# Dilated attention in an encoder layer: heads kept apart by zeros in q's tiles, k whole as hi and lo, staging in two buffers

## The chip, the cores and the metric

The kernel runs on one core of a Trainium2 chip. The metric is the device time of one execution in microseconds, the median of several runs. Engines are named as in the profile: PE is the matrix engine (TensorE), PEld its weight loads, DVE the vector engine, ACT the scalar engine, POOL is GpSimd, SP the engine that issues most DMAs.

## What is computed

One encoder layer over 2048 positions of width 1024, all in float32: a mixer of three parallel head groups, cross-attention into 256 memory tokens, and a gated feed-forward block with a convolution of width 3. The change lies in the third head group of the mixer, the dilated window attention. It has three groups of two heads of 64 columns each, with dilations 1, 4 and 16; each query sees the keys at most 64 steps of its dilation away:

```python
def _dilated_window_attention(q, k, v, rel_table_g, dilation, radius):
    ...
    logits = jnp.einsum('bdnqhe,bdnkhe->bdnhqk', qs, kb).astype(jnp.float32) * (E ** -0.5)
    logits = logits + bias[None, None, None].astype(jnp.float32)
    logits = jnp.where(valid[None, None, :, None], logits, NEG_INF)
    lse = jax.nn.logsumexp(logits, axis=-1)
    p = jnp.exp(logits - lse[..., None]).astype(v.dtype)
    out = jnp.einsum('bdnhqk,bdnkhe->bdnqhe', p, vb).reshape(B, dilation, Lp, H, E)[:, :, :L]
    ...
```

The three groups' outputs are merged with weights from their softmax denominators.

## The kernel before

The program runs four stages one after the other. `mix_in` projects the input and writes q, k and the pooling channels, transposed, to `zt` in DRAM and v to `vt`. `mixer` does the dilated attention and, between its pieces, the projections of the memory tokens (`kv_step`). `OutProj` and `xattn` follow, then `Ffn`. Every product is made from float32 operands that are split into a rounded part (hi, type F32R) and its remainder (lo); `mm3` (lines 111 to 117) adds the three products hi*hi, hi*lo and lo*hi in PSUM.

In `mixer` the attention is cut into 12 units: three groups, dilation 16 (g = 2) first, then 4, then 1, with four units of 512 queries each. A unit holds 512 keys for g = 2 and 640 (64 more at each side) for the others. `unit` (line 894) loads and splits a unit's operands, and `block` (line 956) computes 128 queries against 256 keys, for two heads; for g = 2 a block is two sets of 128 queries against 128 keys. So a unit has four blocks (two for g = 2), and there are 32 blocks of 256-wide products and 8 blocks of twice as many 128-wide ones. One unit ahead is prepared while a unit's blocks run (line 1072); its split tiles alternate between two pools, `un[0]` and `un[1]`, by the unit's number.

How `unit` splits its operands: the transposed k of two heads arrives as one tile of 128 partitions, head 0 on partitions 0 to 63, head 1 on 64 to 127. For each head, `kh` is made to hold that head's hi twice, on both halves of the partitions: ACT writes one half (line 924), DVE copies the other (line 925, through `copy`, line 873), and DVE makes the remainder `kl` on 64 partitions (line 926). `q` holds, for each head, hi on the lower half and lo on the upper half (lines 930 to 934), with one more DVE copy for head 1. So one product over 128 rows gives hi*hi and lo*hi together, and a second over 64 rows gives hi*lo:

```python
nc.tensor.matmul(pl[:, a, ws], q[:, a, qs], kh[:, a, ks], start=True, stop=False)
nc.tensor.matmul(pl[:, a, ws], q[lo, a, qs], kl[:, a, ks], start=False, stop=True)
```

After them DVE adds the bias and finds the row's maximum (line 975), ACT takes the exponent (980), PE transposes (985), ACT and DVE split the result (988, 989), PE multiplies by v (999), and ACT and DVE gather the output (1003, 1004). `merge` (1008) joins the three groups.

`stage` (line 907) loads a tile through SP's queue; its pool `m_stg` has one buffer for each of the tags sk, sq and sv, so the next unit's load waits until the last reader of this unit's tile is done. `kv_step` (line 1121) loads weights by SP as well (line 1088), and POOL splits them (`split_w`, lines 95 and 99). The framework orders the instructions of each engine itself, by a simulated time line, so their order is not that of the source; each engine then runs its own list strictly in order.

Of the kernel before, what the change touches and what calls it, by code (L numbers as in the profile page):

```python
# [9 lines left out]
F32 = mybir.dt.float32  # L10
F32R = mybir.dt.float32r
I32 = mybir.dt.int32
AF = mybir.ActivationFunctionType
ALU = mybir.AluOpType
# [4 lines left out]
P = 128  # L19
# [807 lines left out]


MJ = 2
KD_ENG, QD_ENG = "dve", "dve"  # L830
KVH, KVL = ("pool",), ("pool",)
OEB, LGB, PHB = 6, 4, 2
UJ = (3, 2, 1)
# [3 lines left out]
def mixer(cx, zt, vt, yt, tt, mem, mem_t, gm, w_kv, w_qt, w_o, gx, a_d, vo_d, open_proj):  # L837
# [4 lines left out]
    tc, nc = cx.tc, cx.nc  # L842
    with ExitStack() as es:
        ek = ExitStack()
        pool = cx.pools(ek)
# [3 lines left out]
        kvp = pool("m_kv", 2, side="right")  # L849
        psk = pool("m_psk", 2, space=PSUM, side="right")  # L850
        pool = cx.pools(es)
        stg = pool("m_stg", 1)
        midp = pool("m_mid", 2)
        un = [pool("m_un0", 1)]
        one = pool("m_one", 1)
# [8 lines left out]
        pso = pool("m_pso", 2, space=PSUM)  # L864


        og = {g: dr.tile([S, 132], F32, name=f"og{g}") for g in (1, 2)}

        def copy(eng, out, src, f):
            if eng == "act":  # L870
                nc.scalar.activation(out, src, AF.Copy, scale=f)
            else:
                (nc.gpsimd if eng == "pool" else nc.vector).tensor_scalar(out, src, f, 1.0, op0=ALU.mult, op1=ALU.mult)

        def mask_tiles(g):

# [17 lines left out]
        def unit(g, u, masks):  # L894

            d = DIL[g]
            L = S // d
            pad = 0 if d == 16 else 64  # L900
            n = 512 + 2 * pad
            c0 = 512 * u

            z0 = pad if (g == 1 or u == 0) else 0
            z1 = n - pad if (g == 1 or u == 3) else n

            def stage(b, pd, tag):
                w = 512 + 2 * pd
                y0, y1 = (z0, z1) if pd else (0, w)
                t = stg.tile([P, w], F32, name="stage", tag=tag)  # L910
                for lo, hi in ((0, y0), (y1, w)):
                    if lo < hi:
                        nc.vector.memset(t[:, lo:hi], 0.0)
                nc.sync.dma_start(t[:, y0:y1], zt[b, :, c0 - pd + y0:c0 - pd + y1])
                return t


            lo, up = slice(0, 64), slice(64, P)
            heads = (lo, up)
            s = stage(5 + g, pad, "sk")  # L920
            kh = un[u % 2].tile([P, 2, n], F32R, name="kh", tag="kh")
            kl = un[u % 2].tile([64, 2, n], F32R, name="kl", tag="kl")
            for a, h in enumerate(heads):
                nc.scalar.activation(kh[h, a], s[h], AF.Copy)
                copy(KD_ENG, kh[heads[1 - a], a], s[h], 1.0)
                nc.vector.tensor_tensor(kl[:, a], s[h], kh[h, a].bitcast(F32), op=ALU.subtract)
            s = stage(2 + g, 0, "sq")
            q = un[u % 2].tile([P, 2, 512], F32R, name="q", tag="q")
            for a, h in enumerate(heads):
                nc.scalar.activation(q[h, a], s[h], AF.Copy, scale=0.125)  # L930
                if a:
                    copy(QD_ENG, q[lo, a], s[h], 0.125)
                nc.vector.scalar_tensor_tensor(q[up, a], s[h], 0.125, q[h, a].bitcast(F32),
                                               op0=ALU.mult, op1=ALU.subtract)

            nt = n // P
            s = stg.tile([P, nt, P], F32, name="stage", tag="sv")
            rows = vt[:, g * P:(g + 1) * P].rearrange("(l r) c -> r l c", r=d)
            if g == 2:
                nc.sync.dma_start(s, rows[4 * u:4 * u + 4].rearrange("r l c -> l r c"))  # L940
            else:
                rows, k0 = rows[u if g == 1 else 0], (0 if g == 1 else c0) - pad
                t0, t1 = int(z0 > 0), nt - (z1 < n)
                if t0:
                    nc.vector.memset(s[:64, 0], 0.0)
                    nc.sync.dma_start(s[64:, 0], rows[:64])
                if t1 < nt:
                    nc.vector.memset(s[64:, t1], 0.0)
                    nc.sync.dma_start(s[:64, t1], rows[L - 64:])
                nc.sync.dma_start(s[:, t0:t1], rows[k0 + t0 * P:k0 + t1 * P].rearrange("(t p) c -> p t c", p=P))  # L950
            v = un[u % 2].tile([P, nt, 2, 2, 64], F32R, name="v", tag="v")
            s4 = s.rearrange("p t (a e) -> p t a e", a=2)
            nc.scalar.activation(v[:, :, :, 0], s4, AF.Copy)
            nc.vector.tensor_tensor(v[:, :, :, 1], s4, v[:, :, :, 0].bitcast(F32), op=ALU.subtract)

            def block(i, oe):

                pl = psl.tile([P, 2, 256], F32, name="pl", tag="pl")
                if g == 2:

                    parts = [(slice((2 * i + j) * P, (2 * i + j + 1) * P),) * 2 + (slice(j * P, (j + 1) * P), j)
                             for j in range(2)]
                    mk = masks[1]
                else:
                    parts = [(slice(i * P, (i + 1) * P), slice(i * P, (i + 2) * P), slice(0, 256), 0)]
                    first, last = (i == 0, i == 3) if g == 1 else (u == 0 and i == 0, u == 3 and i == 3)
                    mk = masks[0 if first else 2 if last else 1]
                for a in range(2):
                    for qs, ks, ws, _ in parts:
                        nc.tensor.matmul(pl[:, a, ws], q[:, a, qs], kh[:, a, ks], start=True, stop=False)  # L970
                        nc.tensor.matmul(pl[:, a, ws], q[lo, a, qs], kl[:, a, ks], start=False, stop=True)
                lg = lgp.tile([P, 2, 256], F32, name="lg", tag="lg")
                for a in range(2):
                    for _, _, ws, j in parts:
                        nc.vector.tensor_tensor_reduce(out=lg[:, a, ws], in0=pl[:, a, ws], in1=mk[:, a, ws], scale=-1.0,
                                                       scalar=3e38, op0=ALU.add, op1=ALU.min,
                                                       accum_out=oe[:, j, 128 + a:129 + a])
                for a in range(2):
                    for _, _, ws, j in parts:
                        nc.scalar.activation(lg[:, a, ws], lg[:, a, ws], AF.Exp, scale=-1.0,  # L980
                                             bias=oe[:, j, 128 + a:129 + a], accum_out=oe[:, j, 130 + a:131 + a])
                pt = psp.tile([P, 4, P], F32, name="pt", tag="pt")
                for a in range(2):
                    for t in range(2):
                        nc.tensor.transpose(pt[:, 2 * a + t], lg[:, a, t * P:(t + 1) * P], cx.ident)
                ph = wk.tile([P, 4, P], F32R, name="ph", tag="ph", bufs=PHB)
                pl_ = wk.tile([P, 4, P], F32R, name="pl_", tag="pl_", bufs=PHB)
                nc.scalar.activation(ph, pt, AF.Copy)
                nc.vector.tensor_tensor(pl_, pt, ph.bitcast(F32), op=ALU.subtract)
                m = len(parts)  # L990

                po = pso.tile([P, 2, 2, 2, 64], F32, name="po", tag="po")
                for j in range(m):
                    for a in range(2):
                        ts = [j] if g == 2 else [0, 1]
                        for t in ts:
                            vi = 2 * i + t if g == 2 else i + t
                            for p in (ph, pl_):
                                nc.tensor.matmul(po[:, j, a].rearrange("p h e -> p (h e)"), p[:, 2 * a + t],
                                                 v[:, vi, a].rearrange("p h e -> p (h e)"),  # L1000
                                                 start=t == ts[0] and p is ph, stop=t == ts[-1] and p is pl_)
                o4 = oe[:, :, 0:128].rearrange("p m (a e) -> p m a e", a=2)
                nc.scalar.activation(o4, po[:, :m, :, 0], AF.Copy)
                nc.vector.tensor_tensor(o4, o4, po[:, :m, :, 1], op=ALU.add)

            return block
# [102 lines left out]
        for i in range(2):  # L1109
# [4 lines left out]
            for k in range(4):  # L1114
# [3 lines left out]
                                               op0=ALU.mult, op1=ALU.subtract)  # L1118
# [299 lines left out]
def body(tc, x_t, gmix, w_t, b_t, w_v, b_v, w_a, b_a, v_g, w_s, b_s, rel, oh, mrow, pw, pb, psc, edge, invw, mem, mem_t, gm, w_kv, w_qt,  # L1418
         w_o, gmem, w_out, b_out, b_o, w_up, b_up, conv, w_down, b_down, gffn, gfin, out):
    with tc.tile_pool(name="const", bufs=1) as const, tc.tile_pool(name="scratch", bufs=1, space=DRAM) as dr:  # L1420
# [15 lines left out]
        def open_proj():  # L1436
# [4 lines left out]
            return proj[0].chunk  # L1441

        mixer(cx, zt, vt, yt, tt, mem, mem_t, gm, w_kv, w_qt, w_o, gmem, a_d, vo_d, open_proj)
        with late, ExitStack() as ef, ExitStack() as ep:
            def ffn():
# [55 lines left out]
```

## Time and profile before

| | us |
|---|---|
| median of 3 runs | 2616.39 (2615.14 to 2619.52) |
| the profiled execution | 2622.29 |
| its span in the trace | 2620.5 |

| stretch of the trace (us) | what runs | PE busy | DVE busy | granted clock |
|---|---|---|---|---|
| 0 to 430 | input projections, gating, pooling | 412.8 | 287.7 | 0.98 to 1.00 |
| 430 to 712 | dilated attention and the memory projections | 251.1 | 227.0 | 0.88 |
| 712 to 1010 | output projection, cross-attention begins | 286.8 | 192.4 | 0.97 to 0.99 |
| 1010 to 2620 | the rest of it and the feed-forward block | 1569.6 | 1162.2 | 0.99 |

The granted clock is the share of full speed that the chip allowed PE, on average over the stretch; it has two levels, 1.2 and 2.4 GHz, so 0.88 is a mixture of 0.5 and 1. A matmul's duration includes its way through the array, so two neighbours overlap in the records; what a matmul costs is the distance from its start to the next one's start.

### The profile page before, as it was taken

How to read it: one execution, taken by the hardware profiler on the slowest of the kernel's cores; microseconds unless marked ns; L12 is line 12 of the kernel's file. 1: busy time of each engine (PE TensorE's matmuls, PEld its weight loads, DVE VectorE, ACT ScalarE, POOL GpSimd, SP SyncE). 2: the span in 40 equal slices, each digit the busy share in tenths (PEclk: the TensorE clock that was granted, in tenths of full speed). 3: DMA queues.
4: the chain of work that ended last, by engine and by line, in shares of the span. 5: the costliest groups of instructions: out<-in, count | busy, mean ns of one | idle time of the engine just before them, and what ended most of it. 6: DMA issues, size and time to landing. Idle time of an engine off the chain costs nothing. (4 is left out here: it accounts for less than half of the span.)

```text
span 2620.5 us, 33979 instructions
## 1 busy us (share of the span) xinstructions
PE 2520.3 (96%) x12390; PEld 2137.0 (82%) x12390; DVE 1869.3 (71%) x2736; ACT 1010.1 (39%) x1536; POOL 1017.4 (39%) x841
## 2 busy tenths in 40 slices
PE   8999998899999899998999999989999999999998
PEld 6988896787778799987788888767888888888886
DVE  7666748878763967667788888785888887646453
ACT  4222112556321333323444444443444444444442
POOL 5233314555211332335755555243655654201100
PEclk9999998799999999998999999999999999999998
DMA  6334427565574122223222222574222223767673
GB/s 210 116 102 140 142 69 219 173 188 168 173 255 151 56 73 69 69 77 109 81 81 81 80 89 81 185 231 139 73 81 89 73 83 103 264 210 238 216 236 122
DMA packets 217791, 353.18 MB, mean 135 GB/s; under 512 B 38572, under 2 KB 104216, under 8 KB 217624
## 3 DMA queue, kind: packets, MB, share of 16 engines
q1 hardware_dynamic: 153676, 278.44, 34.0%
q10 hardware_dynamic: 63948, 72.58, 7.9%
q8 instruction: 97, 1.59, 0.3%
q14 instruction: 70, 0.57, 0.1%
HBM read 272.22 MB, written 79.90 MB: 134 GB/s over the span
## 5 line engine op out<-in xcount | busy, mean ns | idle before, releaser
L362 DVE TENSOR_TENSOR w<-dr,w 128x1024 fp32r<-128x1024 f32 x176 | 223.5, 1277 | 172.8 <-ACT w L361 167.4
L116 PE MATMUL pd<-w 128*128 128x512 f32 x704 | 276.6, 393 | 10.8 <-DVE w L362 10.8
L117 PE MATMUL pd<-w 128*128 128x512 f32 x704 | 275.4, 391 | 0.0
L361 ACT ACTIVATE w<-dr 128x1024 fp32r<-128x1024 f32 x176 | 184.9, 1058 | 217.6 <-PE pd L117 198.7
L115 PE MATMUL pd<-w 128*128 128x512 f32 x704 | 265.1, 392 | 0.0
L115 PE MATMUL py<-hth,w 128*128 128x512 f32 x528 | 208.0, 396 | 1.5 <-DVE u L333 1.5
L116 PE MATMUL py<-htl,w 128*128 128x512 f32 x528 | 207.7, 393 | 0.0
L117 PE MATMUL py<-hth,w 128*128 128x512 f32 x528 | 206.0, 394 | 0.0
L277 DVE SCALAR_TENSOR_TENSOR t<-u,vec,t 128x1022 f32<-128x1022 f32 (+1 forms) x88 | 132.5, 1506 | 69.6 <-ACT t L276 47.6
L276 ACT ACTIVATE t<-u,vec 128x1022 f32<-128x1022 f32 (+1 forms) x88 | 109.6, 1245 | 159.7 <-DVE u L326 139.6
L116 PEld LDWEIGHTS pd<-w 128*128 128x128 f32 x704 | 132.8, 189 | 40.6 <-DVE w L362 13.4
L115 PEld LDWEIGHTS pd<-w 128*128 128x128 f32 x704 | 132.8, 189 | 27.8 <-ACT w L361 0.4
L117 PEld LDWEIGHTS pd<-w 128*128 128x128 f32 x704 | 133.0, 189 | 27.4
L421 POOL TENSOR_TENSOR q<-q 128x512 f32<-128x512 f32 x24 | 39.6, 1650 | 273.7 <-ACT q L417 272.6
L115 PE MATMUL px<-hth,w 128*128 128x512 f32 x352 | 140.4, 399 | 1.6 <-DVE xd L403 1.6
L116 PE MATMUL px<-htl,w 128*128 128x512 f32 x352 | 139.5, 396 | 1.5 <-POOL htl L197 1.5
L117 PE MATMUL px<-hth,w 128*128 128x512 f32 x352 | 139.7, 397 | 0.4 <-DVE w L228 0.4
L115 PE MATMUL pz<-hth,w 128*128 128x512 f32 x352 | 139.8, 397 | 0.0
L117 PE MATMUL pz<-hth,w 128*128 128x512 f32 x352 | 138.9, 395 | 0.0
L278 DVE SCALAR_TENSOR_TENSOR t<-u,vec,t 128x1022 f32<-128x1022 f32 (+1 forms) x88 | 138.6, 1576 | 0.1
L116 PE MATMUL pz<-htl,w 128*128 128x512 f32 x352 | 138.4, 393 | 0.0
L234 POOL TENSOR_TENSOR ws<-wb 128x512 f32<-128x512 f32 x44 | 63.4, 1440 | 177.9 <-DVE w L228 119.7
(714 smaller groups left out, 7280.3 us busy)
## 6 DMA issues: line engine op xcount, KB each, us to landing
dr<-act_d SPq DMA_DIRECT2D x176, 256.0 KB, 3.7
dr<-in_w_down_dram SPq DMA_DIRECT2D x176, 256.0 KB, 4.0
wa<-in_w_up_dram SPq DMA_DIRECT2D x44, 512.0 KB, 3.2
wb<-in_w_up_dram SPq DMA_DIRECT2D x44, 512.0 KB, 3.2
st<-in_w_t_dram SPq DMA_DIRECT2D x32, 512.0 KB, 3.7
xt<-in_x_t_dram SPq DMA_DIRECT2D x56, 256.0 KB, 3.8
act_d<-t ACTq DMA_DIRECT2D x22, 513.0 KB, 2.7
act_d<-t ACTq DMA_DIRECT2D x22, 511.0 KB, 3.0
```

Source lines behind the costliest of these rows:

```text
L115: mm(out, a[0], b[0], start=start, stop=False, skip_group_check=again)
L116: mm(out, a[0], b[1], start=False, stop=False, skip_group_check=again)
L117: mm(out, a[1], b[0], start=False, stop=stop, skip_group_check=again)
L234: tt(s[:, 0], b[:, 0], b[:, 1], op=ALU.add)
L276: nc.scalar.activation(t, u[:, 1:n + 1], AF.Identity, bias=vec[:, 4, f:f + 1], scale=vec[:, 2, f:f + 1])
L277: nc.vector.scalar_tensor_tensor(t, u[:, 0:n], vec[:, 1, f:f + 1], t, op0=ALU.mult, op1=ALU.add)
L278: nc.vector.scalar_tensor_tensor(t, u[:, 2:n + 2], vec[:, 3, f:f + 1], t, op0=ALU.mult, op1=ALU.add)
L361: nc.scalar.activation(hl[:, 0], t, AF.Copy)
L362: nc.vector.tensor_tensor(hl[:, 1], t, hl[:, 0].bitcast(F32), op=ALU.subtract)
L421: nc.gpsimd.tensor_tensor(sq[0], sq[0], q, op=ALU.add)
```

## The change

k is kept whole: `kh` and `kl` are one tile each of 128 partitions, both heads in their own halves, made by one ACT and one DVE instruction. The heads are kept apart on q's side: two fixed tiles `qz`, one for either parity of the unit, hold for each head a hi and a lo tile of 128 partitions in which the other head's half is zero. The zeros are written once, by four POOL memsets of 64 partitions and 1024 columns, when the stage is set up. The DVE copies of k and q are gone, and with them the helper `copy`. Each logit tile is now made by `mm3`: three products over 128 rows in place of one over 128 and one over 64. `m_stg` has two buffers for each tag.

```diff
 MJ = 2
-KD_ENG, QD_ENG = "dve", "dve"
...
-        stg = pool("m_stg", 1)
+        stg = pool("m_stg", 2)
...
+        qz = [un[i].tile([P, 2, 2, 512], F32R, name=f"q{i}") for i in range(2)]
+        for t in qz:
+            nc.gpsimd.memset(t[:64, 1].bitcast(F32), 0.0)
+            nc.gpsimd.memset(t[64:, 0].bitcast(F32), 0.0)
+
...
-        def copy(eng, out, src, f):
-            if eng == "act":
-                nc.scalar.activation(out, src, AF.Copy, scale=f)
-            else:
-                (nc.gpsimd if eng == "pool" else nc.vector).tensor_scalar(out, src, f, 1.0, op0=ALU.mult, op1=ALU.mult)
...
-            lo, up = slice(0, 64), slice(64, P)
-            heads = (lo, up)
             s = stage(5 + g, pad, "sk")
-            kh = un[u % 2].tile([P, 2, n], F32R, name="kh", tag="kh")
-            kl = un[u % 2].tile([64, 2, n], F32R, name="kl", tag="kl")
-            for a, h in enumerate(heads):
-                nc.scalar.activation(kh[h, a], s[h], AF.Copy)
-                copy(KD_ENG, kh[heads[1 - a], a], s[h], 1.0)
-                nc.vector.tensor_tensor(kl[:, a], s[h], kh[h, a].bitcast(F32), op=ALU.subtract)
+            kh = un[u % 2].tile([P, n], F32R, name="kh", tag="kh")
+            kl = un[u % 2].tile([P, n], F32R, name="kl", tag="kl")
+            nc.scalar.activation(kh, s, AF.Copy)
+            nc.vector.tensor_tensor(kl, s, kh.bitcast(F32), op=ALU.subtract)
             s = stage(2 + g, 0, "sq")
-            q = un[u % 2].tile([P, 2, 512], F32R, name="q", tag="q")
-            for a, h in enumerate(heads):
-                nc.scalar.activation(q[h, a], s[h], AF.Copy, scale=0.125)
-                if a:
-                    copy(QD_ENG, q[lo, a], s[h], 0.125)
-                nc.vector.scalar_tensor_tensor(q[up, a], s[h], 0.125, q[h, a].bitcast(F32),
+            q = qz[u % 2]
+            for a, h in enumerate((slice(0, 64), slice(64, P))):
+                nc.scalar.activation(q[h, a, 0], s[h], AF.Copy, scale=0.125)
+                nc.vector.scalar_tensor_tensor(q[h, a, 1], s[h], 0.125, q[h, a, 0].bitcast(F32),
                                                op0=ALU.mult, op1=ALU.subtract)
...
-                        nc.tensor.matmul(pl[:, a, ws], q[:, a, qs], kh[:, a, ks], start=True, stop=False)
-                        nc.tensor.matmul(pl[:, a, ws], q[lo, a, qs], kl[:, a, ks], start=False, stop=True)
+                        cx.mm3(pl[:, a, ws], (q[:, a, 0, qs], q[:, a, 1, qs]), (kh[:, ks], kl[:, ks]), True, True)
```

## Rows read from the trace of the kernel before

**Rows 1.** The page's first line.
```profile
span 2620.5 us, 33979 instructions
```

**Rows 2.** Busy time by stretch (stretch, length, PE, PEld, DVE, ACT, POOL, clock, DMA).
```profile
430.00:712.00 282.00, 251.11 (x1447) 214.41 (x1447) 227.03 (x520) 153.93 (x420) 134.03 (x86) 0.88 0.58 180
...
1010.00:2620.00 1610.00, 1569.61 (x7307) 1302.22 (x7305) 1162.18 (x1290) 682.43 (x829) 659.69 (x522) 0.99 0.39 127
```

**Rows 3.** Time line of PE, a block of 256-wide logits (columns: start, duration, what).
```profile
584.27 0.36 PE L970 MATMUL pl<-kh,q 128*128 128x256 f32 x1
584.57 0.38 PE L971 MATMUL pl<-kl,q 64*128 64x256 f32 x1
...
585.50 0.33 PE L999 MATMUL po<-v,ph 128*128 128x128 f32 x1
```

**Rows 4.** Time line of PE: line 970 with a full-height neighbour; seven memory-projection products.
```profile
530.12 0.28 PE L970 MATMUL pl<-kh,q 128*128 128x256 f32 x1
530.24 0.22 PE L999 MATMUL po<-v,ph 128*128 128x128 f32 x1
...
597.11 0.28 PE L116 MATMUL pt<-ml,kwh 128*128 128x256 f32 x1
...
597.82 0.28 PE L116 MATMUL pt<-ml,kwh 128*128 128x256 f32 x1
```

**Rows 5.** Line 970: its products by shape (ns: least, median, longest).
```profile
L970 PE MATMUL pl<-kh,q x96: 221/382/582, 446.7 to 685.7; 128*128 128x256 f32 x64, 128*128 128x128 f32 x32
```

**Rows 6.** Time line of PE: eight 128-wide logits; nine 128-wide products with v.
```profile
462.17 0.33 PE L970 MATMUL pl<-kh,q 128*128 128x128 f32 x1
...
464.21 0.39 PE L115 MATMUL pt<-kvh,kwh 128*128 128x256 f32 x1
...
505.17 0.28 PE L999 MATMUL po<-v,ph 128*128 128x128 f32 x1
...
506.06 0.28 PE L999 MATMUL po<-v,ph 128*128 128x128 f32 x1
```

**Rows 7.** Busy time of line 873 alone, then of line 926 alone (DVE).
```profile
430.00:712.00 282.00, 29.92 (x36) 0.88 0.58 180
...
430.00:712.00 282.00, 26.88 (x24) 0.88 0.58 180
```

**Rows 8.** Lines 873 and 926 (ns: least, median, longest); a 128-row subtraction on DVE.
```profile
L873 DVE TENSOR_SCALAR kh<-stage x24: 420/489/2592, 439.3 to 644.7; 64x640 fp32r<-64x640 f32 x16, 64x512 fp32r<-64x512 f32 x8
...
L926 DVE TENSOR_TENSOR kl<-stage,kh x24: 673/815/2933, 441.9 to 647.3; 64x640 fp32r<-64x640 f32 x16, 64x512 fp32r<-64x512 f32 x8
...
529.90 0.82 DVE L954 TENSOR_TENSOR v<-stage,v 128x640 fp32r<-128x640 f32 x1
```

**Rows 9.** PE's first and last wait behind unit preparation, and DVE's work before each.
```profile
451.25 2.92 DVE L873 TENSOR_SCALAR kh<-stage 64x512 fp32r<-64x512 f32 x2
...
455.86 0.58 PE L116 MATMUL pt<-kvl,kwh 128*128 128x256 f32 x1 [2.07 <-DVE kvl L1132]
...
630.88 2.21 DVE L873 TENSOR_SCALAR q<-stage 64x512 fp32r<-64x512 f32 x1
...
637.89 0.58 PE L970 MATMUL pl<-kh,q 128*128 128x256 f32 x1 [2.10 <-DVE e L975]
```

**Rows 10.** Time line of PE inside 14 logits in a row, no wait between.
```profile
492.58 0.32 PE L971 MATMUL pl<-kl,q 64*128 64x128 f32 x1
...
493.19 0.47 PE L971 MATMUL pl<-kl,q 64*128 64x128 f32 x1
```

**Rows 11.** POOL: a memset of 128 columns; its idle time before a weight split.
```profile
L890 POOL MEMSET mk<- x4: 204/205/206, 443.8 to 615.0; 128x128 f32 x4
...
368.98 1.06 POOL L95 TENSOR_SCALAR wth<-st 128x1024 fp32r<-128x1024 f32 x1 [38.61 <-PE pz L116]
```

**Rows 12.** Waits of SP's queue, 430 to 712 us (total, times, longest).
```profile
SPq L914 <- DVE kl L926: 41.4, 9, 7.6
SPq L914 <- DVE q L933: 28.0, 10, 6.5
```

## Prediction

> **What bounds the kernel now.** I read the page first, then busy time by stretch, then PE's waits and time line in the one stretch that the change touches, 430 to 712 us. The span is 2620.5 us [rows 1]; the profiled execution took 2622.29 us, so 1.8 us lie outside it, and the median of the runs, 2616.39 us, is 5.9 us below that execution. I work out a difference inside the trace and apply it to both.
>
> Behind the stretch, from 1010 us on, PE is busy 1569.6 of 1610 us [rows 2]. PE's list is the spine of the program; what the attention stage saves on PE's path moves all that follows and reaches the end one for one.
>
> Inside the stage PE is busy 251.1 of 282 us, DVE 227.0, ACT 153.9, POOL 134.0 [rows 2]. PE is the nearest to full, and it loses time in three ways that busy time hides or shows: products that start too far apart, 30.9 us of idle time (282 less 251.1), and a granted clock of 0.88, which is 68 us at the lower of its two levels (2 x 0.12 x 282). The change can act on each.
>
> **Part 1, the logits on PE.** The reader is to look at starts, not durations. A block of four 256-wide logits runs from 584.27 to 585.50 us, 1.23 us [rows 3], 0.31 apiece. But where line 970 meets a neighbour over all 128 rows, that one starts 0.12 us later (530.12 to 530.24) [rows 4]. So the product itself is not slow; the change of height between 128 and 64 rows is, and it is paid at almost each start. Memory-projection products of the same shape, three to a sum as the new logits will be, run seven starts in 0.71 us, 0.118 apart [rows 4]. The new block has six: 0.71 us, 0.52 less. There are 64 products of line 970 of that width, two heads to a block, so 32 blocks [rows 5]: 32 x 0.52 = 16.6 us.
>
> The 128-wide ones: eight take 462.17 to 464.21, 2.04 us; products of 128 columns that all have 128 rows start 0.111 apart (nine from 505.17 to 506.06) [rows 6]. Twelve of them take 1.33 us, 0.71 less; 32 products of line 970 [rows 5] are eight such blocks: 5.7 us. Together 22 us less of PE's time. Ends: 0, if the third product costs what the change of height gives back, and 24, if part of the stage stays at the lower clock, where both numbers grow. I take 22, since each of its rows is of the same shape as what it stands for.
>
> **Part 2, DVE.** Twelve units lose three copies each (36 instructions of line 873, 29.9 us as they ran) and half of the 24 subtractions of line 926 (26.9 us, so 13.4) [rows 7], since 128 rows cost what 64 do: 0.82 against 0.815 us [rows 8]. That is 43 us; at least 25, going by the least copy (36 x 0.42) and the median subtraction (12 x 0.815) [rows 8], because many of them ran two to five times longer than that beside POOL's weight splits. ACT loses one of two activations per unit on k; ACT is busy 153.9 of 282 us [rows 2], so that is worth nothing by itself.
>
> What reaches PE: six of PE's waits on DVE stand directly behind such work in DVE's list, the first 2.07 us at 455.86 behind two copies of 2.92 us, the last 2.10 us at 637.89 with a copy of 2.21 us ahead [rows 9]; the six make 13.6 us. The rest of the 30.9 us stands behind work that stays. I take 10 of the 13.6, as q's own splits and v's stay in the list and run beside the same POOL splits. Ends: 0, if another instruction is late instead, and 19, with the waits next to them.
>
> **Part 3, the clock.** It falls after waits, and also without one: in a row of 14 logits with no wait a product went from 0.32 to 0.47 us at 493 us [rows 10]. Of 68 us at the lower level half, 34, is lost where PE had work. Fewer waits and denser logits should give some back. I take 5; ends 0 and 17 (half of the loss). The Trainium skill, "TensorE: Matmul & The Clock Gate", section "Why this matters for your kernels", asks for no idle gaps between bursts and does not say that a busy but sparse stretch loses the clock too. By it alone only the waits of part 2 would count here, and the sum would be 2 to 3 us smaller; the row at 493 us speaks for counting the logits as well.
>
> **Part 4, what is added or moved.** The four zero-writes are POOL memsets of 1024 columns; a 128-column one takes 0.204 us, so at most 1.63 each, 6.5 us together [rows 11]. POOL idles up to 38.6 us at a time before this stage [rows 11], which covers them. POOL's list is strict: if a zero-write waits for memory that `mix_in` still uses, the weight splits behind it wait, and then PE for those. That would cost up to 10 us, once, at about 430 us; it is in the range. The second staging buffer frees SP: its queue stood 41.4 us for the readers of k's tile and 28.0 for q's [rows 12], with weight loads queued behind. Little of that reaches PE, because the splits of those weights mostly wait for PE to free their buffer. I take 0; ends 0 and 5 us gained. Two more loads in flight cost nothing where DMA is busy 0.58 of the time [rows 2].
>
> **Part 5, cover lost.** While PE ran the slow logits, the chain of the softmax (DVE, ACT, PE, ACT, DVE, PE) went on. With 22 us less to run, PE meets some of its ends earlier. The order is also planned anew by the framework, so the filling between them changes. PE idles 30.9 us beside 251.1 of work now, an eighth; I charge a third of part 1, 8 us, more than that eighth because the memory projections that fill the gaps are not more than before. Ends 0 and 22.
>
> **Sum.** 22 + 10 + 5 - 8 = 29 us less: 2593 for an execution like the profiled one, and 2616.4 - 29 = 2587 us for the median.
>
> **Rivals.**
>
> *The filling runs out.* Part 1's gain comes back whole as waits behind DVE and ACT, and only a few us of part 2 remain: -22 + 22, with -2 or so, 2611 to 2620, say 2614. For it: DVE is busy 227 of 282 us, and all of PE's long waits in the stage name it. Against it: DVE loses at the same time 25 to 43 us, more than PE does. Chance 0.13.
>
> *The third product costs a full step (slower).* If products against k's lo also start 0.31 us after their neighbour, or 0.255 for the narrow ones, the change adds 64 x 0.31 + 32 x 0.255 = 28 us to PE; less 10 from part 2 that is +18, 2634 us. It turns at 0.205 us a product for the wide ones (two thirds of 0.31). Against it stands the start after 0.12 us [rows 4]. Chance 0.05.
>
> *The narrow products were nearly free.* The Trainium skill, "TensorEngine Tiling (Array Packing)", sections "The Solution" and "Theoretical Speedup", says that products over at most 64 rows can run in separate halves of the array, up to twice as fast; padding them with zeros gives that up. As a mechanism of this kernel: the 64-row products would lie beside their neighbours, and the change would then add three full products for one. By the rows' steps that is 64 x 0.118 + 32 x 0.111 = 11 us more on PE, less 10 from part 2: +1, 2617 us. The trace denies it here, since the start that follows a 64-row product is always late [rows 3]. Chance 0.02.
>
> *The clock (slower).* Shorter logits leave PE more short waits, and the clock falls more often. Each us at the lower level costs half a us; if another 90 of the stage's us fall to it, 45 are lost, against 33 from parts 1 and 2 with nothing lost elsewhere: +12, 2628 us. It decides from 66 more us on, twice what was gained. For it: the clock is at 0.88 in this stage with an eighth of idle time. Against it: 90 more would be more than now in all. Chance 0.06.
>
> **How the numbers follow.** The forecast has what is left, 0.74, at 2587 us. 0.2% is 5.2 us, about what a measurement of this kernel can tell from no change. Faster by more: 0.74 and a fourth of the first rival, 0.77. Within: the rest of that rival and the one on narrow products, 0.12. Slower: 0.11. The range: the ends of the parts give 24 + 19 + 17 + 5 with nothing lost, 2551 us, and with the cover lost in full and the POOL wait, about 2616; not all ends meet, so 2560 at the bottom, and 2616 at the top, which takes in most of the first rival.
>
> **What would show it.** Right: in the trace of the changed kernel the six products of a block start 0.12 us apart at full clock; lines 873 and 926 shrink to 12 subtractions; DVE's busy time in the stage falls by 25 to 43 us; the stage, from its first memory projection to its last logits, is about 29 us shorter, its clock above 0.90, and the stretch behind it keeps its length. SP's waits on stage buffers are gone without PE noticing. Wrong: product starts of 0.2 us and more (part 1), PE's idle time in the stage above 35 us (part 5), waits of PE for POOL near the stage's start (part 4), or a shift of more than a few us before or behind the stage, which none of this accounts for.

## The result, and the profile after

The changed kernel takes 2581.5 us (median; 2579.25 to 2584.01), against 2615.76 us for the kernel before beside it: a ratio of 0.9867, 95% interval 0.985 to 0.9884. That is 34 us less, where 29 were forecast (2587 us, range 2560 to 2616). Its profiled execution took 2579.88 us.

The page of after, first line and section 1 (busy time, share of the span, instructions):

```profile
span 2578.1 us, 34129 instructions
...
PE 2486.3 (96%) x12486; PEld 2125.4 (82%) x12486; DVE 1823.8 (71%) x2688; ACT 1000.5 (39%) x1524; POOL 1015.6 (39%) x845
```

The span is 42.4 us shorter than in [rows 1]. Of these, the profile of before was 5.9 us above its own median, so the span overstates the gain; I look for the place by stretch. The cuts are events that both kernels have: the last product of `mix_in` (`pz`), the first product of the step behind the output projection (`pl<-am0h`), and the first of the FFN (`px`). Between the first two cuts lies the attention stage with its output projection. Busy time by stretch (stretch, length, then PE, PEld, DVE, ACT, POOL with their instructions, granted clock, DMA share, GB/s), of before:

```profile
430.50:833.13 402.63, 367.43 (x1957) 309.20 (x1956) 285.68 (x638) 171.25 (x445) 151.87 (x98) 0.91 0.59 187
...
833.10:1232.00 398.90, 380.73 (x2401) 345.30 (x2401) 287.38 (x748) 121.07 (x268) 140.18 (x152) 0.98 0.26 81
```

and of after:

```profile
429.90:795.32 365.42, 335.30 (x2053) 300.74 (x2052) 241.20 (x590) 161.30 (x433) 151.34 (x102) 0.94 0.66 206
...
795.32:1194.10 398.78, 380.33 (x2400) 345.09 (x2401) 287.11 (x748) 121.12 (x268) 140.17 (x152) 0.98 0.26 80
```

All that counts is in the first pair: 37.2 us less. The stretch ahead of it moved by 0.6 us, the one behind kept its length to 0.1, and the last one, which has no changed line, is 4.5 us shorter (1388.5 to 1384.0). That is no gain of the change: over the 14 kernels measured here this last stretch, which none of them touches, is 1381 to 1389.5 us long.

The 37.2 us can be parted. PE's idle time is length less busy. Twice (1 - clock) times length is time at the lower of the two levels, and half of it is lost. What is left is PE's work as it would run at full clock: busy less that half. Before: idle 35.2, lower level 72, work 331. After: idle 30.1, lower level 44, work 313. So **18 us less work, 14 us of lost clock got back, 5 us less waiting**. The clock has two decimals here, and kernels with the same work come out up to 5 us apart below, so a few us are open between the first two. And 37.2 us, from one profile of each kernel, is 3 us more than the 34 of the medians.

PE's time line of after at a block of 256-wide logits, where [rows 3] had four products in 1.23 us (start, duration, what):

```profile
573.96 0.28 PE L115 MATMUL pl<-kh,q 128*128 128x256 f32 x1
574.08 0.28 PE L116 MATMUL pl<-kl,q 128*128 128x256 f32 x1
574.20 0.28 PE L117 MATMUL pl<-kh,q 128*128 128x256 f32 x1
...
574.67 0.28 PE L115 MATMUL pl<-kh,q 128*128 128x256 f32 x1
...
446.13 0.28 PE L116 MATMUL pl<-kl,q 128*128 128x128 f32 x1
...
448.59 0.28 PE L117 MATMUL pl<-kh,q 128*128 128x128 f32 x1
```

Six products, 573.96 to 574.67: 0.71 us. The last two lines bound 22 starts of the 128-wide kind, in 2.46 us: 0.112 apart. No product stands out as late, those against k's lo included.

DVE's lines of unit preparation in after (least/median/longest ns, first and last start), and POOL's zero-writes:

```profile
L921 DVE TENSOR_TENSOR kl<-stage,kh x12: 671/823/1644, 439.8 to 623.6; 128x640 fp32r<-128x640 f32 x8, 128x512 fp32r<-128x512 f32 x4
...
L926 DVE SCALAR_TENSOR_TENSOR q<-stage,q x24: 672/1176/2840, 440.4 to 622.2; 64x512 fp32r<-64x512 f32 x24
...
L869 POOL MEMSET q<- x2: 946/948/950, 425.1 to 443.5; 64x1024 f32 x2
```

The copies of line 873 are gone, and k's 24 subtractions are 12, each as long at 128 rows as it was at 64 (823 against 815 ns [rows 8]). DVE's busy time in the stretch fell by 44.5 us.

### The profile page after: what moved, and what is told of

It reads as the page before. It is cut to its first block, busy times and chain, and to the rows that moved or that the text cites. A ratio compares the mean times of both kernels' runs of the same rounds, so it can differ in the third digit from the quotient of the medians.

```text
span 2578.1 us, 34129 instructions
## 1 busy us (share of the span) xinstructions
PE 2486.3 (96%) x12486; PEld 2125.4 (82%) x12486; DVE 1823.8 (71%) x2688; ACT 1000.5 (39%) x1524; POOL 1015.6 (39%) x845
```

## The experiments

The forecast added up parts that it took as independent: faster logits on PE (part 1) and a lighter DVE (part 2). The theories in the quoted texts are letters for who carries the gain: H, the change of height on PE alone; D, DVE's load alone; S, the second staging buffer; B, both engines together, neither being worth much alone; F, a third product that helps of itself; K, a cost of writing k's hi in halves. Where nothing else is said, a stretch is the one between the first two cuts. The runs came in three groups with a kernel before of their own (2614.93, 2616.5 and 2621.65 us), so I compare ratios; after's, 0.9867, was measured beside the 2615.76 us above. The forecasts in the quoted texts are in us of a kernel before at about 2616.

The runs with what they leave in the stretch, worked out as above (us; from one profile each):

| kernel | ratio [95%] | stretch | PE work | PE idle | lower level | DVE busy |
|---|---|---|---|---|---|---|
| before | 1 | 402.6 | 331 | 35 | 72 | 286 |
| after | 0.9867 [0.985, 0.9884] | 365.4 | 313 | 30 | 44 | 241 |
| height_only | 1.0053 [1.0036, 1.0069] | 411.7 | 299 | 63 | 99 | 294 |
| act_copies | 1.0028 [1.0013, 1.0043] | 401.2 | 335 | 35 | 64 | 263 |
| less_dve | 0.9983 [0.9968, 0.9998] | 394.2 | 335 | 28 | 63 | 249 |
| dve_back | 0.9984 [0.9968, 0.9999] | 392.0 | 314 | 51 | 55 | 287 |
| two_full_act | 0.998 [0.9968, 0.9992] | 393.3 | 304 | 58 | 63 | 268 |
| less_dve_two | 0.9946 [0.9926, 0.9966] | 384.6 | 304 | 46 | 69 | 263 |
| less_dve_three | 0.9886 [0.9869, 0.9903] | 377.7 | 312 | 43 | 45 | 250 |
| stg_one | 0.9893 [0.9871, 0.9914] | 366.7 | 317 | 35 | 29 | 243 |
| height_half | 0.9906 [0.9883, 0.9928] | 376.3 | 331 | 27 | 38 | 246 |
| kh_halves | 0.9878 [0.9862, 0.9895] | 371.6 | 313 | 36 | 45 | 251 |
| four | 0.9874 [0.9859, 0.9888] | 369.4 | 328 | 30 | 22 | 251 |
| v_on_pool | 0.9886 [0.9868, 0.9903] | 370.4 | 318 | 34 | 37 | 238 |

**height_only: part 1 alone, in the kernel before.** k's lo gets 64 zero rows, written once, so that both products stand at 128 rows; DVE's work stays. A logit keeps two products, where after has three; dve_back below has the three.

```diff
+        klz = [un[i].tile([P, 2, 640], F32R, name=f"kl{i}") for i in range(2)]
+        for t in klz:
+            nc.gpsimd.memset(t[64:].bitcast(F32), 0.0)
...
-            kl = un[u % 2].tile([64, 2, n], F32R, name="kl", tag="kl")
+            kl = klz[u % 2]
...
-                        nc.tensor.matmul(pl[:, a, ws], q[lo, a, qs], kl[:, a, ks], start=False, stop=True)
+                        nc.tensor.matmul(pl[:, a, ws], q[:, a, qs], kl[:, a, ks], start=False, stop=True)
```

> The kernel before with one thing changed: the second product of a logit runs over all 128 rows instead of 64. kl gets 128 partitions whose upper half is zero for good (two fixed tiles, two POOL memsets), and q is used whole. Still two products per logit, all DVE copies as before, one staging buffer. Theory H (the change of height is what made the logits slow): starts 0.118 us apart for the wide ones and 0.111 for the narrow ones, so a wide block takes 0.47 us instead of 1.23 (32 blocks, 24 us) and a narrow one 0.89 instead of 2.04 (8 blocks, 9 us): 33 us of PE's work gone, some more by the clock, a third back as waits since DVE is untouched: 2585 us, between 2575 and 2597. Theory D (the gain came from taking copies off DVE): PE's waits on DVE fill what the logits leave, 2606 to 2616 us. Theory S (the second staging buffer did it): about 2616 us.

2628.11 us, 1.0053: slower by 13 us, which none of the three theories had. PE's work did fall as priced, by 32 us (331 to 299). None of it reached the end: idle time rose by 28 us, and the lower level took 27 more. Line 973 is 970 of before. DVE's time line during PE's longest wait on it (start, duration, what, [idle before <- releaser]):

```profile
450.22 2.97 DVE L876 TENSOR_SCALAR kh<-stage 64x512 fp32r<-64x512 f32 x2 [0.40 <-DMA stage<-zt]
453.11 1.25 DVE L876 TENSOR_SCALAR q<-stage 64x512 fp32r<-64x512 f32 x1
454.40 3.43 DVE L929 TENSOR_TENSOR kl<-stage,kh 64x512 fp32r<-64x512 f32 x2
457.86 0.99 DVE L730 TENSOR_SCALAR yo<-pp,pvec 128x256 f32<-128x256 f32 x2
458.77 0.42 DVE L1135 TENSOR_TENSOR kvl<-pt,kvh 128x256 fp32r<-128x256 f32 x1
```

PE's time line around that wait:

```profile
452.15 0.35 PE L115 MATMUL pt<-kvh,kwh 128*128 128x256 f32 x1 [0.80 <-ACT kvh L1134]
459.24 0.58 PE L116 MATMUL pt<-kvl,kwh 128*128 128x256 f32 x1 [6.73 <-DVE kvl L1135]
459.62 0.42 PE L117 MATMUL pt<-kvh,kwl 128*128 128x256 f32 x1
459.84 0.41 PE L115 MATMUL pt<-kvh,kwh 128*128 128x256 f32 x1
460.05 0.41 PE L116 MATMUL pt<-kvl,kwh 128*128 128x256 f32 x1
```

The memory projection's `kvl`, 0.42 us of work, stands in DVE's list behind 8.6 us of work, 7.65 of them (2.97 + 1.25 + 3.43) the copies and subtractions that the change takes away or halves. PE waits 6.73 us, and behind the wait the products start 0.21 us apart where they start 0.118 apart otherwise [rows 4], and the granted clock from 459.2 to 463.9 us is 0.51, the lower level: the wait is paid a second time in the clock. This is the mechanism of the rival "the filling runs out", true where PE's logits alone get faster.

**less_dve: part 2 alone, in the kernel before.** The copies and the second head's subtraction on k are left out (tiles zeroed once), the products stay at their heights.

```diff
-                copy(KD_ENG, kh[heads[1 - a], a], s[h], 1.0)
-                nc.vector.tensor_tensor(kl[:, a], s[h], kh[h, a].bitcast(F32), op=ALU.subtract)
...
+                if a == 0:
+                    nc.vector.tensor_tensor(kl[:64, a, :n], s[h], kh[h, a, :n].bitcast(F32), op=ALU.subtract)
...
-                if a:
-                    copy(QD_ENG, q[lo, a], s[h], 0.125)
```

> The kernel before, with DVE's load cut to that of the changed kernel and nothing else gained: the three copies per unit and one of the two subtractions are left out (so the output is not the reference's: the copied halves of k and q and head 1's lo of k stay zero). Two products per logit with the change of height, one staging buffer. Theory H (PE's pace of the logits carries the gain by itself) would have this near the kernel before, 2603 to 2616 us, but height_only has shown that the pace alone gives nothing. Theory D (DVE's load by itself): 2580 to 2590 us. Theory B (both together: PE and DVE hand the stage's time to each other, and either saving alone turns into waiting for the other): 2600 to 2616 us, PE's idle time in the stage 10 us lower at most.

0.9983: 4 us, at the bound of what can be told from nothing, with 37 us of DVE's work gone and 7 us less idle time on PE, as B had it. Theory D falls. That PE's spread-out logits had covered DVE's work fits these numbers.

**act_copies: DVE relieved by moving the copies to ACT, in the kernel before.**

```diff
-KD_ENG, QD_ENG = "dve", "dve"
+KD_ENG, QD_ENG = "act", "act"
```

> The kernel before with one thing changed: the three copies of k and q per unit are made by ACT instead of DVE (36 instructions, 30 us of DVE as they ran in the kernel before). The logits' products and the staging stay. Theory H: PE's work is the same, only waits behind those copies go, at most 13 us and more likely 5: 2605 to 2615 us. Theory D: most of the measured gain of 34 us comes, 2580 to 2597 us. Theory S: about 2616 us.

1.0028: 7 us slower, which none of the theories had, though DVE has 23 us less to do; ACT has 25 more (171 to 196 us). The profiled execution was the fastest of its twelve (2616.46 us against a median of 2623.62), and its stretch is 1.4 us shorter than before's, so where the 7 us lie isn't shown. Here, what DVE dropped was no gain once ACT had to do it.

**dve_back: after with DVE's old load put back** as work that nobody reads, so that PE runs the new logits beside the old DVE.

```diff
-            nc.vector.tensor_tensor(kl, s, kh.bitcast(F32), op=ALU.subtract)
+            dum = un[u % 2].tile([64, 640], F32R, name="dum", tag="dum")
+            for h in (slice(0, 64), slice(64, P)):
+                nc.vector.tensor_scalar(dum[:, :n], s[h], 1.0, 1.0, op0=ALU.mult, op1=ALU.mult)
+                nc.vector.tensor_tensor(kl[h], s[h], kh[h].bitcast(F32), op=ALU.subtract)
             s = stage(2 + g, 0, "sq")
+            nc.vector.tensor_scalar(dum[:, :512], s[64:], 0.125, 1.0, op0=ALU.mult, op1=ALU.mult)
```

> The changed kernel with DVE's old load put back: per unit the subtraction for k in two halves and three copies of the old shapes into a tile that nobody reads. Products and staging as in the changed kernel. Theory H: 2 to 13 us slower than the changed kernel, 2584 to 2594 us. Theory D: most of the gain is lost, 2603 to 2616 us. Theory S: about 2582 us.

0.9984: of after's 34 us, 30 are gone, as D had it here, though D fell with less_dve. Its row of the stretch, and that of less_dve:

```profile
428.50:820.51 392.01, 341.13 (x2053) 305.11 (x2052) 286.63 (x638) 161.75 (x433) 156.50 (x102) 0.93 0.61 193
...
430.20:824.44 394.24, 366.23 (x1958) 306.62 (x1956) 248.57 (x590) 171.10 (x445) 153.68 (x103) 0.92 0.60 192
```

PE's wait list of dve_back's stretch (us in total, times, longest us) shows where PE now waits:

```profile
PE pt L115 <- DVE kvl L1128: 20.4, 5, 6.1
...
PE pt L116 <- DVE kvl L1128: 2.4, 1, 2.4
```

Before has of the same kind:

```profile
PE pt L116 <- DVE kvl L1132: 3.2, 2, 2.1
...
PE pt L115 <- DVE kvl L1132: 1.7, 1, 1.7
```

and after:

```profile
PE pt L115 <- DVE kvl L1124: 3.8, 1, 3.8
...
PE pt L116 <- DVE kvl L1124: 2.1, 1, 2.1
```

With dve_back's third (0.8 us, line 117) that is 23.6, against 4.9 and 5.9 us. height_only's three sums make 22.6. So this wait is long in both kernels in which PE's logits are full-height and DVE keeps its whole load; in the other twelve it is at most 11.1 us (four).

Four kernels now answer the question by themselves: neither part, 1 (before); after's logits beside DVE's old load, 0.9984 (dve_back); before's logits beside the light DVE, 0.9983 (less_dve); both, 0.9867 (after). **Either part alone is worth 4 us, both together 34.** In that, B stands. dve_back and after also have the second staging buffer and fewer ACT instructions; stg_one and kh_halves below ask for their worth.

**two_full_act: height_only with the copies on ACT and two staging buffers.** Its edits are those above and `pool("m_stg", 2)`.

> A version that computes everything: height_only with the copies of k and q made by ACT and two staging buffers. PE does two products of full height per logit (33 us less than before), DVE loses 30 us of copies and keeps both subtractions, ACT gains 25 us. Theory B: both fall, so the gain comes, 2575 to 2592 us. Theory D: act_copies showed that moving the copies to ACT gives nothing, so about 2610 to 2628 us. Theory H: 2580 us.

0.998, in D's range and not in B's. Better than height_only by 19 us, 30 behind after: DVE is still at 268 us, ACT at 195, PE idle 58.

**less_dve_two: less_dve, both products at 128 rows, two staging buffers.** Two products where after has three.

```diff
-        stg = pool("m_stg", 1)
+        stg = pool("m_stg", 2)
...
-                        nc.tensor.matmul(pl[:, a, ws], q[lo, a, qs], kl[:64, a, ks], start=False, stop=True)
+                        nc.tensor.matmul(pl[:, a, ws], q[:, a, qs], kl[:, a, ks], start=False, stop=True)
```

> The same load of DVE as the changed kernel (copies and one subtraction left out, so the output is not the reference's), two staging buffers, and both products of a logit over 128 rows: the changed kernel but for two products instead of three. PE has 64 x 0.118 + 32 x 0.111 = 11 us less to do than in the changed kernel. Theory B: some of it arrives, 2570 to 2582 us. Theory D (DVE's load alone decides): as the changed kernel within 4 us, 2578 to 2586 us. Theory H: the 11 us arrive whole, 2568 to 2573 us.

0.9946 (2603.68 us): faster than either part alone, yet 20 us behind after, which has a product more in each logit, and above the range of every theory (2586 us at the most). Its DVE ran longer (263 us), and its lower level is 69 us, close to before's 72.

**less_dve_three: the same with the second product issued twice**, which is after's amount of work on both engines.

```diff
                         nc.tensor.matmul(pl[:, a, ws], q[:, a, qs], kh[:, a, ks], start=True, stop=False)
+                        nc.tensor.matmul(pl[:, a, ws], q[:, a, qs], kl[:, a, ks], start=False, stop=False)
                         nc.tensor.matmul(pl[:, a, ws], q[:, a, qs], kl[:, a, ks], start=False, stop=True)
```

> less_dve_two with a third product of full height per logit (the second one is added twice, so this output too is not the reference's, and the copies and one subtraction stay left out). PE then has exactly the changed kernel's work, DVE too; what still differs is k's hi in two ACT instructions instead of one (9 us more of ACT in all). less_dve_two was 22 us slower than the changed kernel although PE had 11 us less to do. Theory F (the third product itself helps: with it PE's list, as the framework plans it, has work where it waited before, and the clock stays up): 2580 to 2592 us, that is faster than less_dve_two with more work. Theory K (the halved k costs that much, through ACT and the start of each unit): 2603 to 2616 us. Plain cost of PE's work: 2610 to 2615 us.

0.9886: 8 us more work on PE, about 16 us less time, and not to be told from after. The lower level falls from 69 to 45 us, idle time from 46 to 43, DVE's busy time from 263 to 250.

**four: after with a fourth product, q's lo against k's lo.**

```diff
-                        cx.mm3(pl[:, a, ws], (q[:, a, 0, qs], q[:, a, 1, qs]), (kh[:, ks], kl[:, ks]), True, True)
+                        cx.mm3(pl[:, a, ws], (q[:, a, 0, qs], q[:, a, 1, qs]), (kh[:, ks], kl[:, ks]), True, False)
+                        nc.tensor.matmul(pl[:, a, ws], q[:, a, 1, qs], kl[:, ks], start=False, stop=True)
```

> The changed kernel with a fourth product per logit, lo of q with lo of k, at full height: 64 x 0.118 + 32 x 0.111 = 11 us more of PE's work, nothing else touched. If PE's work in this stage is what the stage is made of (theories H and B): 8 to 14 us slower, 2589 to 2596 us. Theory F: less than half of it, 2580 to 2586 us.

0.9874, within after's interval and 2 us behind it by the medians, where H and B had 8 to 14. 15 us more work (313 to 328) cost nothing that can be measured; the lower level is 22 us, half of after's 44. So B's other half, that PE's work is what the stage is made of, isn't borne out. The clock of the stretch is the third number from the right in its row. less_dve_two, two products to a logit:

```profile
430.60:815.22 384.62, 338.19 (x1958) 298.96 (x1956) 262.89 (x590) 170.20 (x445) 161.44 (x104) 0.91 0.61 196
```

less_dve_three, three products:

```profile
430.90:808.62 377.72, 334.50 (x2054) 299.07 (x2052) 249.59 (x590) 169.34 (x445) 153.75 (x104) 0.94 0.64 200
```

four, four products:

```profile
429.10:798.47 369.37, 339.45 (x2149) 305.03 (x2148) 251.19 (x590) 161.57 (x433) 154.54 (x102) 0.97 0.64 205
```

0.91, 0.94, 0.97. The whole table sorts the same way: the six kernels with two products to a logit have 63 to 99 us at the lower level, the seven with three have 29 to 55, the one with four 22, and DVE's load doesn't move any of them out of its group (dve_back, with three products and a loaded DVE, has 55). That the extra product pays for itself in clock is what these rows suggest. But the framework plans the order anew for every kernel, and PE's lists of these three differ far beyond the logits, so the plan's part and the clock's part aren't separated here. That stays open.

**height_half: after with the first head's middle product cut back to 64 rows**, whose other rows are zeros anyway; the second head keeps 128.

```diff
-                        cx.mm3(pl[:, a, ws], (q[:, a, 0, qs], q[:, a, 1, qs]), (kh[:, ks], kl[:, ks]), True, True)
+                        mm, r = nc.tensor.matmul, slice(0, P if a else 64)
+                        mm(pl[:, a, ws], q[:, a, 0, qs], kh[:, ks], start=True, stop=False)
+                        mm(pl[:, a, ws], q[r, a, 0, qs], kl[r, ks], start=False, stop=False)
+                        mm(pl[:, a, ws], q[:, a, 1, qs], kh[:, ks], start=False, stop=True)
```

> The changed kernel, but the middle product of head 0 (hi of q with lo of k) runs over 64 rows again; its zeros lie in the other half, so the result is the same. Only the change of height comes back, for half of the logits; DVE and ACT are untouched. By the steps of the kernel before each such pair costs about 0.27 us more for wide blocks and 0.2 for narrow ones: 32 x 0.27 + 16 x 0.2 = 12 us of PE. Theories H and B: 6 to 14 us slower than the changed kernel, 2588 to 2597 us. Theory D: as the changed kernel within 4 us.

0.9906, 10 us slower than after by the medians (the intervals just touch), 10.9 by the stretch, with the same number of products and half of the rows in one of six. PE's time line of one block, both heads:

```profile
507.05 0.38 PE L964 MATMUL pl<-kh,q 128*128 128x256 f32 x1 [0.40 <-DVE oe L970]
507.36 0.38 PE L965 MATMUL pl<-kl,q 64*128 64x256 f32 x1
507.68 0.39 PE L966 MATMUL pl<-kh,q 128*128 128x256 f32 x1
507.90 0.28 PE L964 MATMUL pl<-kh,q 128*128 128x256 f32 x1
508.02 0.28 PE L965 MATMUL pl<-kl,q 128*128 128x256 f32 x1
508.13 0.28 PE L966 MATMUL pl<-kh,q 128*128 128x256 f32 x1
```

The triple with one short product takes 0.85 us here, the full one 0.35 (508.02 less 507.90, three times). This block starts behind a wait; over all triples that the time line shows one by one, the medians are 0.79 us against 0.36 for the wide ones and 0.62 against 0.34 for the narrow ones. So two changes of height cost 0.43 and 0.28 us, in the changed kernel too (0.27 and 0.2 were expected), and 32 x 0.43 + 16 x 0.28 = 18 us is what PE's work rose by (313 to 331). Of these, 10 reached the end.

This shows by itself what a change of height costs. It isn't all that PE's side brings. less_dve has much the same PE work (335 against 331 us), DVE load (249 against 246) and idle time (28 against 27), and yet it is 20 us slower than height_half (0.9983 against 0.9906); what differs is the lower level, 63 against 38 us. From less_dve on, equal heights with the second buffer bring 10 us (less_dve_two) and the third product 16 more (less_dve_three), by a way that isn't separated. Both heads at 64 rows wasn't tried.

**stg_one, kh_halves, v_on_pool: the rest of the change, one at a time, in after.** One staging buffer; k's hi written in two halves on ACT; v's lo subtraction moved from DVE to POOL.

```diff
-        stg = pool("m_stg", 2)
+        stg = pool("m_stg", 1)
```

> The changed kernel with one staging buffer per tag, as before the change. Theories H and D: within 5 us of the changed kernel, 2577 to 2587 us, as SP's waits for the readers of the stage reach PE nowhere. Theory S: 2600 us or more.

```diff
-            nc.scalar.activation(kh, s, AF.Copy)
+            for h in (slice(0, 64), slice(64, P)):
+                nc.scalar.activation(kh[h], s[h], AF.Copy)
```

> The changed kernel with k's hi made by two ACT instructions of 64 partitions instead of one of 128: 12 more ACT instructions of about 0.7 us, 9 us of ACT. Theory K: 10 to 22 us slower than the changed kernel, 2591 to 2604 us. Theories B and F: within 4 us of it, as ACT is busy 161 of 365 us there.

```diff
-            nc.vector.tensor_tensor(v[:, :, :, 1], s4, v[:, :, :, 0].bitcast(F32), op=ALU.subtract)
+            nc.gpsimd.tensor_tensor(v[:, :, :, 1], s4, v[:, :, :, 0].bitcast(F32), op=ALU.subtract)
```

> The changed kernel with v's lo (12 subtractions of 128 partitions, 0.8 us each when undisturbed) made by POOL instead of DVE. dve_back showed that 45 us of DVE's time cost 30 us here. Theories B and D: 10 to 15 us less of DVE gives up to 10 us, 2571 to 2582 us, if POOL's weight splits behind them aren't late. Theory H: as the changed kernel within 4 us, 2577 to 2586 us.

0.9893, 0.9878 and 0.9886, by the medians 7, 3 and 5 us behind after; the interval of each overlaps after's. S and K aren't supported: neither the buffer nor the one activation carries anything that can be told from nothing. The gain of up to 10 us that B and D gave v_on_pool didn't come. The twelve subtractions of v (11.9 us on DVE in after) brought POOL from 151 to 172 us, while DVE's busy time fell only from 241 to 238: what DVE still had to do ran longer. No version here beats after.

## Why the prediction was right, and where its steps were not

**Where and how much: right.** The time went from the stretch that was named, the one behind it kept its length, and the size (34 against 29) lies well inside the range. Slower was given 0.11, and none of its mechanisms came for the whole change. (One slip there: parts 1 and 2 make 32 and not 33, so the rival of the clock turns at 64 us and not at 66.) From its first memory projection to its last logits, the length that the prediction named, the stage is 41 us shorter (254.6 to 213.4), not 29; the larger stretch holds the same work in both kernels, but for the third products, and is the better measure. But not every step behind the number holds.

**Part 1, 22 us on PE: right in mechanism, a little large.** The blocks run in 0.71 us as priced, the narrow ones at 0.112 apart, and there is no third product that costs a full step, as that rival had it. Full-clock work fell by 18. height_half shows that it is the change of height that cost. The rival by which short products lie beside their neighbours has nothing for it: shortening one product made its triple 0.79 us instead of 0.36.

**Part 2, DVE: load right, worth mis-sized, and the step wrong.** 43 us were to leave DVE; 44.5 did, just above the upper end. I gave that 10 us at PE, from waits that stood in the trace of before. Those waits are only the ones that stood open beside the logits of before. Beside after's logits the same load is worth 30 us (dve_back), beside before's 4 (less_dve). **The failed step is that parts 1 and 2 were added as if independent.** With DVE as it was, part 1 would have been worth 4 us (dve_back) and not 22 less 8 for lost cover; with two full-height products in place of three it is even 13 us slower (height_only).

**Part 5, cover lost: charged to the wrong thing.** I took 8 us, a third of part 1, whatever DVE did. Beside DVE's old load, after's logits lose nearly all their cover: 17 us less work than before, 16 more of idle time (331 to 314, 35 to 51, dve_back). Beside the light DVE they lose next to none: idle time goes from 28 to 30 (less_dve to after). So 10 of part 2 less 8 of part 5 came to 2 net where 5 were measured; the sum came near by luck, because the two errors lean against each other.

**Part 3, the clock: mis-sized.** 5 us, with an end at 17; measured 28 us less at the lower level, half of it, 14, time. It is the largest miss of the sum (18 + 14 + 5 = 37 against 22 + 5 + 2 = 29). I had reckoned with fewer waits and denser logits. Fewer waits alone don't account for it: dve_back idles 16 us more than before and has 17 us less at the lower level. In the table the lower level goes with the number of products to a logit. The Trainium skill, "TensorE: Matmul & The Clock Gate", section "Why this matters for your kernels", asks for no idle gaps between bursts; height_only agrees (28 us more idle, 27 more at the lower level), dve_back doesn't, and four, as idle as after (30 us) and at 0.97 against 0.94, has a difference that idle time doesn't account for. Why the kernels with more products to a logit have less of it stays open.

**Part 4: nearly nothing, as said, with two small misses.** The zero-writes took 0.95 us or up to 1.12 each, below the 1.63 bound. Two of them run from 443.5 us on and not ahead of the stage; PE's waits for POOL are 1.2 us near the start and 1.8 at 488 us, far from the 10 of the bound. SP's waits on the readers of the staging tiles are not gone, which I had said they would be; they shrank, from 28.0 us for q's tile and 41.4 for k's [rows 12] to

```profile
SPq L913 <- DVE q L926: 21.9, 8, 3.9
SPq L913 <- DVE kl L921: 14.8, 6, 5.1
```

For the second buffer I took 0 with an end at 5. stg_one is 7 us behind after by the medians, with 1.3 us more in the stretch and overlapping intervals, so neither 0 nor 5 is refuted.

**The rival "the filling runs out" (0.13)** deserved its chance for a reason that I gave only as an aside: it is what part 1 does alone (dve_back and height_only). What I held against it, that DVE loses more than PE does, is exactly what decided it. I should have priced the sum in two orders, each part first, and seen that the second one taken is worth more than it shows in the trace of before.

## What to carry to other kernels

When two engines feed each other in one stage, price a change to both as one: a saving on the fuller one brings out the waits behind the other, so what a wait in the trace shows is the worth beside the present pace, and not beside the new one. Measure each part alone before you credit it; here each was worth 4 us alone, and both together 34. Look at distances between starts, not at durations, and keep the rows of neighbouring products alike, with zeros where need be, as long as the zeros are written once.

## What the runs showed of the hardware that I had not expected

- **A product more, no time more.** 15 us more PE work cost nothing that can be measured in four, and 8 us more made less_dve_three about 16 us faster than less_dve_two; the granted clock went 0.91, 0.94, 0.97 with two, three and four products, and all 14 kernels sort by that number. Whether the clock or the new order did it is open.
- **A wait is paid twice.** Behind the 6.73 us wait of height_only the products start 0.21 us apart instead of 0.118, in a row that shows no further wait; the granted clock there is 0.51.
- **The same DVE instruction takes 0.67 to 2.84 us, by what POOL does beside it.** Of q's 64x512 lo subtractions in after, three that met no POOL instruction took 0.67 to 0.69 us (599.68, 620.81 and 622.20 us); the longest, 2.84 us at 467.18, lay beside a weight split (line 99) all along. In total they took 24.9 us before, 31.5 after, 25.2 in less_dve and 20.8 in dve_back, so taking work off DVE can leave the rest longer or not, by where the plan puts it. By v_on_pool, twelve fewer instructions brought DVE 3 us.
